# RMSNorm and QKV product on one core: two head tiles transposed by the DMA crossbar among the weight loads, a new order of the head, and the last columns in halves

## Chip, cores and metric

The kernel runs on one core of a Trainium2 chip. The metric is the device time of one execution in microseconds. Each kernel was run several times, unless the text says otherwise. "Span" is the profiled length of one execution on the core.

## The reference

```python
def reference(x, gamma, w_qkv, eps):          # x: 8 x 1024 x 768, w_qkv: 768 x 2304, f32
    rms = np.sqrt(np.mean(x ** 2, axis=-1, keepdims=True) + eps)
    x_norm = x / rms * gamma
    return np.matmul(x_norm, w_qkv).astype(np.float32)
```

The 8192 rows are 64 tiles of 128 rows. The inner dimension of 768 is six blocks of 128, numbered ko 0 to 5.

## The kernel before

The weights arrive in pieces. Each piece is multiplied by gamma and turned into bf16 ("conv"). A tile of x must stand transposed before it can be the stationary operand. Tiles 0 to 2 are transposed on PE in f32, and tiles 3 to 5 on PE in bf16. From tile 6 on, a DMA crossbar transpose does it, issued by SP:

```python
HEAD = 6                       # tiles that share the weights while these arrive
...
def tr(t):                     # on PE, into PSUM; cp copies it to xT
    PT[t] = psum.tile([P, KO, P], bf16, name="pm")
    for ko in range(KO):
        nc.tensor.transpose(out=PT[t][:, ko, :], in_=XB[t][:, ko * P:(ko + 1) * P], identity=ident)
...
def xbar(t):                   # on the DMA engines
    XT[t] = xTp.tile([P, KO, P], bf16, name="xT")
    nc.sync.dma_start_transpose(out=XT[t], in_=XB[t])
```

1/rms is applied to the product, in the eviction from PSUM. A list gives every operation of the head a planned time, and each engine executes its operations in the order of those times. The times are an order, not waits. After the head, a loop plans one tile after another:

```python
for t in range(HEAD, MT):
    ahead = 6.0 if t < HEAD + 5 else 0.0
    ...
    at(now - 15 - ahead, load_x, t)
    at(now - 8.5 - ahead, cast, t)
    at(now - 7.5 - ahead, xbar, t)
    ...
    for n0 in range(0, N, NT):
        at(now, mm, t, n0, range(KO))
        now += min(NT, N - n0) * US
        flip ^= 1
        evac_at(now + 0.2, t, n0, "DVE" if flip else "ACT", gap=1.2)
```

The line with `ahead` matters later: tiles 6 to 10 have a lead of 6 us, and tile 11 is the first without it. All loads, stores and crossbar transposes but one tiny load are issued by SP, in this order of times.

Of the kernel before, what the change touches and what calls it, by code (L numbers as in the profile page):

```python
# [10 lines left out]
HEAD = 6  # L11
PIECES = [(0, 2, 0, 512), (2, 3, 0, 512), (3, 4, 0, 512), (4, 5, 0, 512), (5, 6, 0, 512), (0, 2,
          512, 512), (2, 4, 512, 512), (4, 6, 512, 512), (0, 2, 1024, 512), (2, 4, 1024, 512), (4,
          6, 1024, 512), (0, 3, 1536, 512), (3, 6, 1536, 512), (0, 6, 2048, 256)]


LOADS = [
    (-9.00, "w", 0), (-8.99, "x", 0), (-8.98, "x", 1), (-8.97, "x", 2), (-8.96, "w", 1),
    (-8.95, "w", 2), (-8.94, "w", 3), (-8.93, "x", 3), (-8.92, "w", 4), (-8.91, "w", 5),
    (-8.90, "x", 4), (-8.89, "w", 6), (-8.88, "w", 7), (-8.87, "x", 5), (-8.86, "w", 8),  # L20
    (-8.85, "w", 9), (-8.84, "w", 10), (-8.83, "w", 11), (-8.82, "w", 12), (-8.81, "w", 13),
    (-8.80, "x", 6), (-8.79, "x", 7),
]

EARLY = 3


HEAD_PLAN = [
    (4.99, "conv", 0, 0, "DVE"), (4.99, "conv", 0, 1, "ACT"), (5.95, "trA", 0), (5.99, "stat", 0),
    (6.82, "trB", 0), (7.04, "trB", 1), (7.18, "cpB", 0, "DVE"), (7.25, "trA", 1),  # L30
    (7.26, "idle", 3), (7.32, "cpA", 0, "ACT"), (7.58, "cpB", 1, "DVE"), (7.94, "stat", 1),
    (7.94, "trA", 2), (7.98, "cpA", 1, "DVE"), (8.37, "mm", 0, 0, "01"),
    (8.65, "conv", 1, 2, "POOL"), (8.66, "cpA", 2, "DVE"), (8.80, "mm", 1, 0, "01"),
    (9.24, "trB", 2), (9.27, "stat", 2), (9.34, "conv", 2, 3, "DVE"), (9.45, "mm", 2, 0, "01"),
    (9.82, "recip", 0), (9.89, "mm", 0, 0, "2"), (9.98, "cpB", 2, "DVE"),
    (9.99, "conv", 3, 4, "POOL"), (10.10, "mm", 1, 0, "2"), (10.32, "mm", 2, 0, "2"),
    (10.38, "recip", 1), (10.53, "mm", 0, 0, "3"), (10.66, "recip", 2), (10.75, "mm", 1, 0, "3"),
    (10.97, "mm", 2, 0, "3"), (10.98, "cast", 3, "DVE"), (10.98, "stat", 3),
    (11.18, "mm", 0, 0, "4"), (11.40, "mm", 1, 0, "4"), (11.61, "tr", 3),
    (11.65, "conv", 4, 5, "DVE"), (11.95, "mm", 2, 0, "4"), (12.13, "cp", 3, "DVE"),  # L40
    (12.19, "mm", 0, 0, "5"), (12.41, "mm", 1, 0, "5"), (12.57, "evac", 0, 0, "ACT"),
    (12.63, "mm", 2, 0, "5"), (12.69, "recip", 3), (12.84, "mm", 3, 0, "012345"),
    (12.85, "evac", 1, 0, "DVE"), (13.26, "conv", 5, 0, "ACT"), (13.60, "conv", 5, 1, "DVE"),
    (13.97, "evac", 2, 0, "ACT"), (14.08, "cast", 4, "DVE"), (14.14, "mm", 0, 512, "01"),
    (14.57, "mm", 1, 512, "0"), (14.63, "evac", 3, 0, "DVE"), (14.66, "stat", 4),
    (14.78, "tr", 4), (15.12, "mm", 1, 512, "1"), (15.33, "conv", 6, 2, "POOL"),
    (15.34, "mm", 2, 512, "01"), (15.38, "cp", 4, "DVE"), (15.77, "mm", 3, 512, "01"),
    (15.99, "conv", 6, 3, "ACT"), (16.05, "recip", 4), (16.20, "mm", 4, 0, "012345"),
    (16.70, "conv", 7, 5, "ACT"), (17.41, "conv", 7, 4, "ACT"), (17.49, "mm", 4, 512, "01"),
    (17.65, "evac", 4, 0, "DVE"), (17.93, "mm", 0, 512, "23"), (18.12, "stat", 5),  # L50
    (18.36, "mm", 1, 512, "23"), (18.40, "cast", 5, "DVE"), (18.79, "mm", 2, 512, "23"),
    (19.01, "conv", 8, 0, "DVE"), (19.22, "tr", 5), (19.49, "conv", 8, 1, "DVE"),
    (19.56, "mm", 3, 512, "23"), (19.97, "cp", 5, "DVE"), (19.99, "mm", 4, 512, "23"),
    (20.42, "mm", 0, 512, "45"), (20.53, "conv", 9, 2, "DVE"), (20.85, "mm", 1, 512, "45"),
    (21.01, "conv", 9, 3, "DVE"), (21.01, "evac", 0, 512, "ACT"), (21.28, "mm", 2, 512, "45"),
    (21.49, "evac", 1, 512, "DVE"), (21.69, "conv", 10, 4, "POOL"), (21.70, "conv", 10, 5, "ACT"),
    (21.71, "mm", 3, 512, "45"), (22.15, "mm", 4, 512, "45"), (22.24, "evac", 2, 512, "DVE"),
    (22.41, "evac", 3, 512, "ACT"), (22.58, "mm", 5, 0, "012345"), (22.99, "evac", 4, 512, "DVE"),
    (23.70, "conv", 11, 1, "ACT"), (23.74, "conv", 11, 2, "DVE"), (23.87, "mm", 5, 512, "012345"),
    (24.22, "conv", 11, 0, "DVE"), (24.70, "recip", 5), (24.92, "evac", 5, 0, "DVE"),  # L60
    (25.17, "mm", 0, 1024, "01"), (25.33, "evac", 5, 512, "ACT"), (25.60, "mm", 1, 1024, "01"),
    (25.71, "conv", 12, 3, "DVE"), (26.02, "conv", 12, 5, "ACT"), (26.03, "mm", 2, 1024, "01"),
    (26.19, "conv", 12, 4, "DVE"), (26.46, "mm", 3, 1024, "01"), (26.89, "mm", 4, 1024, "01"),
    (27.33, "mm", 5, 1024, "01"), (27.76, "mm", 0, 1024, "23"), (28.10, "conv", 13, 1, "ACT"),
    (28.10, "conv", 13, 2, "POOL"), (28.10, "conv", 13, 3, "DVE"), (28.19, "mm", 1, 1024, "23"),
    (28.40, "conv", 13, 5, "DVE"), (28.62, "mm", 2, 1024, "23"), (28.65, "conv", 13, 0, "POOL"),
    (28.70, "conv", 13, 4, "DVE"), (29.05, "mm", 3, 1024, "23"), (29.48, "mm", 4, 1024, "23"),
    (29.91, "mm", 5, 1024, "23"), (30.35, "mm", 0, 1024, "45"), (30.78, "mm", 1, 1024, "45"),
    (30.94, "evac", 0, 1024, "DVE"), (31.21, "mm", 2, 1024, "45"),
    (31.37, "evac", 1, 1024, "ACT"), (31.64, "mm", 3, 1024, "45"),  # L70
    (31.80, "evac", 2, 1024, "DVE"), (32.07, "mm", 4, 1024, "45"),
    (32.23, "evac", 3, 1024, "ACT"), (32.50, "mm", 5, 1024, "45"),
    (32.66, "evac", 4, 1024, "DVE"), (32.94, "mm", 0, 1536, "012"),
    (33.10, "evac", 5, 1024, "ACT"), (33.58, "mm", 1, 1536, "012"), (34.23, "mm", 2, 1536, "012"),
    (34.88, "mm", 3, 1536, "012"), (35.53, "mm", 4, 1536, "012"), (36.17, "mm", 5, 1536, "012"),
    (36.82, "mm", 0, 1536, "345"), (37.47, "mm", 1, 1536, "345"), (37.63, "evac", 0, 1536, "DVE"),
    (38.12, "mm", 2, 1536, "345"), (38.28, "evac", 1, 1536, "ACT"), (38.76, "mm", 3, 1536, "345"),
    (38.92, "evac", 2, 1536, "DVE"), (39.41, "mm", 4, 1536, "345"),
    (39.57, "evac", 3, 1536, "ACT"), (40.06, "mm", 5, 1536, "345"),
    (40.22, "evac", 4, 1536, "DVE"), (40.70, "mm", 0, 2048, "012345"),  # L80
    (40.86, "evac", 5, 1536, "ACT"), (41.36, "mm", 1, 2048, "012345"),
    (41.52, "evac", 0, 2048, "DVE"), (42.02, "mm", 2, 2048, "012345"),
    (42.18, "evac", 1, 2048, "DVE"), (42.67, "mm", 3, 2048, "012345"),
    (42.83, "evac", 2, 2048, "DVE"), (43.33, "mm", 4, 2048, "012345"),
    (43.49, "evac", 3, 2048, "DVE"), (43.98, "mm", 5, 2048, "012345"),
    (44.14, "evac", 4, 2048, "DVE"), (44.80, "evac", 5, 2048, "DVE"),
]
HEAD_END = 44.64


@with_exitstack
def kernel(
# [8 lines left out]
    nc = tc.nc  # L101
# [8 lines left out]
    Kw, N = w_qkv.shape  # L110
# [20 lines left out]

    ctx.enter_context(tc.manual_schedule())

    warm = singles.tile([P, NT], bf16)
    nc.vector.memset(warm, 0.0)  # L135
    g6 = singles.tile([KO, P], f32)
    nc.scalar.dma_start(out=g6, in_=gamma.rearrange("(ko p) -> ko p", p=P))
    eps_sb = singles.tile([P, 1], f32)
# [83 lines left out]

    begun = {}

    def mm(t, n0, kos):
        nl = min(NT, N - n0)
        for ko in kos:
            if (t, n0) not in PM:
                PM[t, n0] = psum.tile([P, NT], f32, name="pm")
            b = begun[t, n0] = begun.get((t, n0), 0) + 1  # L230
            nc.tensor.matmul(out=PM[t, n0][:, :nl], lhsT=XT[t][:, ko, :], rhs=w_b[:, ko, n0:n0 + nl],  # L231
                             start=(b == 1), stop=(b == KO))
# [2 lines left out]
        return max(i for i, (p0, _) in enumerate(PARTS) if p0 <= n0)  # L235

    def evac(t, n0, eng):
        nl = min(NT, N - n0)
        h = part(n0)
        if (t, h) not in OUT:  # L240
            OUT[t, h] = outp.tile([P, PARTS[h][1]], f32, name=f"ot{h}")
        o = OUT[t, h][:, n0 - PARTS[h][0]:n0 - PARTS[h][0] + nl]
        pm = PM[t, n0]
        if eng == "DVE":
            nc.vector.tensor_scalar(out=o, in0=pm[:, :nl], scalar1=RS[t], scalar2=None, op0=mult)  # L245
        else:
            nc.scalar.activation(out=o, in_=pm[:, :nl], func=AF.Copy, scale=RS[t], bias=0.0)  # L247
# [9 lines left out]
    def at(time, fn, *args):  # L257
        plan.append((time, len(plan), fn, args))
# [8 lines left out]
    def evac_at(time, t, n0, eng, gap):  # L267
        at(time, evac, t, n0, eng)
        h = part(n0)
        nl = min(NT, N - n0)  # L270
        left[t, h] = left.get((t, h), PARTS[h][1]) - nl
        if t >= MT - 2:
            at(time + gap - 0.5, store, t, h, n0, nl)
        elif left[t, h] == 0:
            at(time + gap, store, t, h, *PARTS[h])

    def idle(n, nl=P):
        wps = psum.tile([P, NT], f32, name="pm")
        for _ in range(n):
            nc.tensor.matmul(out=wps[:, :nl], lhsT=warm[:, :P], rhs=warm[:, :nl], start=True, stop=True)  # L280


    for time, kind, n in LOADS:
        at(time, {"x": load_x, "w": load_w, "t": xbar}[kind], n)
    at(0.0, idle, 4, NT)
    at(2.8, gamma_in)
    at(2.81, idle, 6, NT)
    at(2.82, idle, 3)
    ops = {"conv": conv, "cast": cast, "stat": stat, "recip": recip, "tr": tr, "cp": cp, "mm": mm, "idle": idle}
    for time, op, *args in HEAD_PLAN:  # L290
        if op == "evac":
# [12 lines left out]
    for t in range(HEAD, MT):  # L304
# [5 lines left out]
        at(now - 7.5 - ahead, xbar, t)  # L310
        at(now - 5, stat, t)
        at(now - 3, recip, t)
        for n0 in range(0, N, NT):
            at(now, mm, t, n0, range(KO))
            now += min(NT, N - n0) * US
            flip ^= 1
            evac_at(now + 0.2, t, n0, "DVE" if flip else "ACT", gap=1.2)

# [37 lines left out]
```

## Time and profile before

| | |
|---|---|
| device time, median of all 6 runs beside the change's | 388.91 us (388.61 to 389.31) |
| span of the profiled run | 386.7 us |
| weight piece 4 (the last of columns 0 to 511) landed | 11.43 us |
| last eviction of the head (tile 5) began | 44.78 us |
| last eviction of the kernel began | 383.21 us |
| time per tile between these | 5.835 us |

Two views of the kernel before that the prediction does not show are needed later. The first is the timeline of PE's weight loads from 66 to 76 us, where tile 11 begins (near 74). Its columns are start, length, engine, line, operation, tile, shapes and count; a wait ahead of a load would follow in brackets:

```profile
65.97 10.04 PEld L231 LDWEIGHTS <-xT 128*128 128x128 bf16 x53
```

One unbroken group: PE waited for nothing there. The second view is the last store on SP (duration, first and last start, then its time to landing):

```profile
L251 SPq DMA_DIRECT2D out_dram<-ot x1: 378/378/378, 383.8 to 383.8; - x1
DMA to landing us min/median/max: 2.0/2.0/2.0
```

It was issued 0.56 us after the last eviction began.

### The profile page before, as it was taken

Reading aid. Unit: us, or ns where it says so; the run is one execution under the profiler, and the core shown is the slowest. Engines: PE = TensorE matmul, PEld = TensorE weight load, DVE = VectorE, ACT = ScalarE, POOL = GpSimd, SP = SyncE. Lnnn points to the kernel's source line nnn. Section 1 sums busy time; section 2 is a strip of 40 time slices with the busy share of each in tenths; the row PEclk is TensorE's granted clock in tenths of the full one; section 3 lists DMA queues with packets and bytes.
Section 4 is the critical chain, followed back from the end, with each engine's and each line's share of the span. In section 5 each row is a group of like instructions: output and inputs, shape, how many; then the busy total and the mean of one; then the engine's idle time right before and its main releaser. Section 6 shows DMA issues by size and latency. Waiting matters only on the chain.

```text
span 386.7 us, 5481 instructions
## 1 busy us (share of the span) xinstructions
PE 380.0 (98%) x1935; PEld 193.1 (50%) x1973; DVE 157.0 (41%) x316; ACT 180.5 (47%) x360; POOL 4.6 (1%) x12
## 2 busy tenths in 40 slices
PE   8999999999999999999999999999999999999996
PEld 5444655454554554554554554554554554554553
DVE  3765543334333344333344333343333343333332
ACT  6743444453544443544444444544444534444532
POOL 1101000000000000000000000000000000000000
PEclk9999999999999999999999999999999999999999
DMA  8999999999998999999999999999999999999975
GB/s 294 390 381 341 394 300 354 325 311 321 287 303 279 307 302 338 313 295 321 283 312 302 303 308 295 316 303 294 311 316 293 297 312 316 288 315 299 279 272 189
DMA packets 87943, 119.52 MB, mean 309 GB/s; under 512 B 50790, under 2 KB 59756, under 8 KB 87916
## 3 DMA queue, kind: packets, MB, share of 16 engines
q1 hardware_dynamic: 87904, 119.17, 101.7%
q8 instruction: 15, 0.25, 0.3%
q14 instruction: 12, 0.10, 0.1%
q10 hardware_dynamic: 12, 0.00, 0.0%
HBM read 32.25 MB, written 75.50 MB: 279 GB/s over the span
## 4 chain that ended last, share of the span: by engine, by line
PE 98%; issue 1%; ACT 0%; DVE 0%
PE pm L231 96%; PE pm L280 1%; PE pm L212 1%; PE pm L198 0%; ACT ot L247 0%; DVE warm L135 0%; PE pm L262 0%; DVE eps_sb L139 0%
## 5 line engine op out<-in xcount | busy, mean ns | idle before, releaser
L231 PE MATMUL pm<-w_b,xT 128*128 128x512 bf16 (+1 forms) x1882 | 372.1, 357 | 2.0
L231 PEld LDWEIGHTS <-xT 128*128 128x128 bf16 x1920 | 187.7, 98 | 184.7 <-DVE xT L174 0.5
L245 DVE TENSOR_SCALAR ot<-pm,rstd 128x512 f32<-128x512 f32 (+1 forms) x164 | 113.4, 693 | 213.0 <-PE pm L231 212.7
L247 ACT ACTIVATE ot<-pm,rstd 128x512 f32<-128x512 f32 (+1 forms) x156 | 101.0, 647 | 192.6 <-PE pm L231 137.4
L185 ACT ACTIVATE sq<-x_t 128x768 bf16<-128x768 f32 x64 | 53.4, 834 | 1.0 <-DMA x_t<-in_x_dram 1.0
L174 DVE CAST xb<-x_t 128x768 bf16<-128x768 f32 x61 | 33.1, 543 | 3.6 <-DMA x_t<-in_x_dram 3.6
L187 ACT ACTIVATE rms<-ssq,eps_sb 128x1 f32<-128x1 f32 x64 | 18.8, 294 | 2.1
L185 ACT ACTIVATION_READ_ACCUMULATOR sq<-x_t 128x1 f32 x64 | 12.3, 192 | 0.0
L192 DVE RECIPROCAL rstd<-rms 128x1 f32<-128x1 f32 x64 | 9.7, 153 | 0.0
L168 ACT ACTIVATE w_b<-w_f,g_sb 128x512 bf16<-128x512 f32 (+1 forms) x9 | 6.1, 693 | 6.1 <-DMA w_f<-in_w_qkv_dram 6.1
L166 DVE TENSOR_SCALAR w_b<-w_f,g_sb 128x512 bf16<-128x512 f32 (+1 forms) x15 | 6.8, 486 | 4.5 <-DMA w_f<-in_w_qkv_dram 4.4
L280 PE MATMUL pm<-warm 128*128 128x512 bf16 (+1 forms) x16 | 5.3, 493 | 1.2 <-DVE eps_sb L139 1.2
L170 POOL TENSOR_SCALAR w_b<-w_f,g_sb 128x512 bf16<-128x512 f32 (+1 forms) x6 | 3.9, 652 | 25.3 <-DMA w_f<-in_w_qkv_dram 25.3
L280 PEld LDWEIGHTS <-warm 128*128 128x128 bf16 x16 | 1.8, 131 | 3.4 <-issue 2.2
L174 DVE CAST xT<-pm 128x256 bf16<-128x256 f32 (+1 forms) x5 | 2.4, 527 | 1.9 <-PE pm L212 1.9
L212 PE MATMUL pm<-ident_f,x_t 128*128 128x128 f32 x18 | 2.8, 300 | 0.0
L212 PEld LDWEIGHTS pm<-ident_f,x_t 128*128 128x128 f32 x18 | 2.4, 162 | 0.2
L142 ACT ACT_TABLE_LOAD x1 | 1.3, 1283 | 1.4 <-PEq L337 1.4
L174 DVE COPY xT<-pm 128x768 bf16<-128x768 bf16 x3 | 1.7, 557 | 0.4 <-PE pm L198 0.4
L198 PEld LDWEIGHTS <-xb 128*128 128x128 bf16 x18 | 1.3, 98 | 0.7
L198 PE MATMUL pm<-ident,xb 128*128 128x128 bf16 x18 | 1.5, 219 | 0.0
L263 DVE COPY g_sb<-pm 128x6 f32<-128x6 f32 x1 | 0.2, 164 | 1.7 <-PE pm L262 1.7
(13 smaller groups left out, 2.7 us busy)
## 6 DMA issues: line engine op xcount, KB each, us to landing
out_dram<-ot SPq DMA_DIRECT2D x124, 512.0 KB, 4.0
x_t<-in_x_dram SPq DMA_DIRECT2D x64, 384.0 KB, 4.4
out_dram<-ot SPq DMA_DIRECT2D x64, 128.0 KB, 3.2
w_f<-in_w_qkv_dram SPq DMA_DIRECT2D x7, 512.0 KB, 7.2
w_f<-in_w_qkv_dram SPq DMA_DIRECT2D x3, 768.0 KB, 9.9
out_dram<-ot SPq DMA_DIRECT2D x8, 256.0 KB, 2.0
w_f<-in_w_qkv_dram SPq DMA_DIRECT2D x4, 256.0 KB, 5.9
xT<-xb SPq DMA_TRANSPOSE x58, 4.5
```

What stands on the lines that cost most here:

```text
L166: nc.vector.tensor_scalar(out=o, in0=i, scalar1=g, scalar2=None, op0=mult)
L168: nc.scalar.activation(out=o, in_=i, func=AF.Copy, scale=g, bias=0.0)
L170: nc.gpsimd.tensor_scalar(out=o, in0=i, scalar1=g, scalar2=1.0, op0=mult, op1=mult)
L174: nc.vector.tensor_copy(out=out, in_=in_)
L185: nc.scalar.activation(out=sq, in_=X[t], func=AF.Square, accum_out=ssq)
L187: nc.scalar.activation(out=rms, in_=ssq, func=AF.Sqrt, scale=inv_k, bias=eps_sb)
L192: nc.vector.reciprocal(out=r, in_=RS[t])
L212: nc.tensor.transpose(out=PT[t, h][:, ko - k0, :], in_=X[t][:, ko * P:(ko + 1) * P], identity=ident_f)
L231: nc.tensor.matmul(out=PM[t, n0][:, :nl], lhsT=XT[t][:, ko, :], rhs=w_b[:, ko, n0:n0 + nl], start=(b == 1), stop=(b == KO))
L245: nc.vector.tensor_scalar(out=o, in0=pm[:, :nl], scalar1=RS[t], scalar2=None, op0=mult)
L247: nc.scalar.activation(out=o, in_=pm[:, :nl], func=AF.Copy, scale=RS[t], bias=0.0)
L280: nc.tensor.matmul(out=wps[:, :nl], lhsT=warm[:, :P], rhs=warm[:, :nl], start=True, stop=True)
```

## The change

The intent is to take work off PE in the head, where PE is already the bound, and to shorten the tail. The diff, cut to its core (the head's list is rewritten whole; four lines stand for it):

```diff
-          6, 1024, 512), (0, 3, 1536, 512), (3, 6, 1536, 512), (0, 6, 2048, 256)]
+          6, 1024, 512), (0, 2, 1536, 512), (2, 4, 1536, 512), (4, 6, 1536, 512), (0, 3, 2048,
+          256), (3, 6, 2048, 256)]
 LOADS = [
...
-    (-8.85, "w", 9), (-8.84, "w", 10), (-8.83, "w", 11), (-8.82, "w", 12), (-8.81, "w", 13),
-    (-8.80, "x", 6), (-8.79, "x", 7),
+    (-8.85, "w", 10), (-8.84, "x", 5), (15.52, "t", 4), (15.53, "w", 11), (15.54, "w", 12),
+    (15.55, "w", 13), (22.65, "t", 5), (22.66, "w", 14), (22.67, "w", 15), (22.68, "x", 6),
+    (22.69, "x", 7),
 ]
 HEAD_PLAN = [        # cut
-    (14.78, "tr", 4), ... (15.38, "cp", 4, "DVE"), ... (19.22, "tr", 5), ... (19.97, "cp", 5, "DVE"),
+    ... (23.66, "mm", 4, 0, "012345"), ... (28.41, "mm", 5, 0, "012345"),
 ]
-    warm = singles.tile([P, NT], bf16)
-    nc.vector.memset(warm, 0.0)
+    ones = nc.const_aps.tensor(1.0, [P, NT], bf16)
...
+    def width(t, n0):
+        return P if t == MT - 1 and n0 >= N - 2 * P else min(NT, N - n0)
...
-    at(0.0, idle, 4, NT)
+    at(0.0, idle, 5, NT)
     at(2.8, gamma_in)
     at(2.81, idle, 6, NT)
-    at(2.82, idle, 3)
...
-        for n0 in range(0, N, NT):
+        for n0 in [*range(0, N, NT)] + [N - P] * (t == MT - 1):
```

"t" in the list of loads is a crossbar transpose, "tr" and "cp" are a transpose on PE and the copy of its result. In the changed kernel the four tiles 0 to 3 consume the first 1024 to 1536 columns, and tiles 4 and 5 follow. A side effect of the list is that the first stores of results come after all of these loads.

## The prediction

> **What bounds the kernel now.** I read the page first, the chain that ended last second, then the timeline of the first 30 us, then transfers (issue time and time to landing) and 1 us windows around the first crossbar transposes.
>
> From the page of the kernel before (busy time, chain, the two costliest kinds):
>
> ```profile
> PE 380.0 (98%) x1935; PEld 193.1 (50%) x1973; DVE 157.0 (41%) x316; ACT 180.5 (47%) x360; POOL 4.6 (1%) x12
> PE 98%; issue 1%; ACT 0%; DVE 0%
> L231 PE MATMUL pm<-w_b,xT 128*128 128x512 bf16 (+1 forms) x1882 | 372.1, 357 | 2.0
> L280 PE MATMUL pm<-warm 128*128 128x512 bf16 (+1 forms) x16 | 5.3, 493 | 1.2 <-DVE eps_sb L139 1.2
> L198 PE MATMUL pm<-ident,xb 128*128 128x128 bf16 x18 | 1.5, 219 | 0.0
> ```
>
> TensorE works to the end: the chain is 98% PE, the matmuls waited 2.0 us in all, and no other engine is above half busy. A busy row is no proof of full speed, so I take the pace from the chain and the evictions. Tile 5's last eviction starts at 44.78, PE's last matmul ends at 383.21: (383.21 - 44.78) / 58 tiles = 5.835 us a tile. A tile has 24 matmuls of 512 columns and 6 of 256, i.e. 27 times 512, so 0.2161 us per 512 columns.
>
> The span is therefore: the time until matmuls run without end, plus everything that PE does besides matmuls after that, plus 64 tiles, plus the tail. Only the first, second and last can change. The chain in order of time shows the second:
>
> ```profile
> 11.75 0.34 PE pm L198 x6
> 12.14 2.75 PE pm L231 x12
> 14.89 0.34 PE pm L198 x6
> 15.23 4.10 PE pm L231 x19
> 19.33 0.34 PE pm L198 x6
> 19.66 1.29 PE pm L231 x6
> ...
> 376.09 7.10 PE pm L231 x38
> 383.21 0.47 ACT ot L247
> ```
>
> (start, length, what.) The three 0.34 pieces are the PE transposes of tiles 3, 4 and 5; no waits of size stand around them. The tail is one ACT eviction, a store that lands 2.0 us after its issue, and the end at 386.7.
>
> What feeds the head is the load stream. Issue times plus times to landing give w piece 4 at 11.43, piece 5 at 12.77, piece 7 at 16.47, piece 9 about 20.1, piece 10 at 23.0, piece 11 at 25.0, piece 12 at 27.05, piece 13 at 29.24, x tiles 6 and 7 at 30.2 and 31.2. That is 524 KB per 1.34 us (391 GB/s), with one jump of about 1.5 us between pieces 9 and 10. The timeline shows the jump at the conversion of piece 10:
>
> ```profile
> 23.02 0.72 ACT L168 ACTIVATE w_b<-w_f,g_sb 128x512 bf16<-128x512 f32 x1 [1.33 <-DMA w_f<-in_w_qkv_dram]
> 23.08 0.69 POOL L170 TENSOR_SCALAR w_b<-w_f,g_sb 128x512 bf16<-128x512 f32 x1 [7.18 <-DMA w_f<-in_w_qkv_dram]
> ```
>
> A 16 KB instruction packet occupies one DMA engine for 1.09 us from 19.59; before it the first and last of the 16 completion marks of a load are 0.75 us apart, after it 2.2. So one engine fell behind and each landing waits for it.
>
> **What the Trainium skill says.** "Runtime: NRT & Kernel Launch", section Instruction fetch mechanics: instructions are refilled in blocks of 16 KiB, 256 instructions, through DMA. The trace agrees in size and spacing: such packets stand at 19.59, 44.3, 65.2, 89.9 us, and PE executes some 256 loads and matmuls in 25 us (255 and 258 in the 50 us from 50). "TensorE: Matmul & The Clock Gate", section on 56 ns against 53.3: warm start-to-start is 55.6 ns at 128 columns and 215.7 at 512. The trace has 0.34 / 6 = 57 ns and 216 ns. "DMA: Bandwidth & Descriptors", section DMA Transpose (X-bar): a transpose next to ordinary transfers needs nothing, two transposing streams must not overlap. All here are issued by SP, so it is one stream. The page gives no cost for one among loads; the trace does, below.
>
> **The change part by part.**
>
> 1. Tiles 4 and 5 leave PE. Removed from PE: two pieces of 0.34, 0.68 us, all on the path. DVE also loses two copies of 0.56, off the path. In their place SP issues two crossbar transposes, costed as a rival below.
>
> 2. The first matmuls. Up to the fourth single-ko piece both kernels wait for the same bytes (the order of loads is the same to piece 5), and 15 matmuls of ko 0 to 4 for three tiles are due before piece 4 is converted. It lands at 11.43, DVE needs 0.49, after the cast of tile 3: ready about 12.0. Before, PE begins ko 5 at 12.14 + 0.22 (tile 2's ko 4 stands behind the transpose) = 12.36, so PE was late by 0.3. After, the fp32 transposes begin when the warm-up ends and all 15 come before tile 3's transpose, with three filler matmuls behind; ko 5 begins about 12.15. Gain 0.2 us.
>
> 3. Constant ones. The memset of 0.27 us goes, PE begins near 0.85 instead of 1.19; warm-up has 11 matmuls of 512 before x instead of 10 and some small ones. At the cold 0.43 us it ends near 5.95 instead of 6.26, just after x tile 0 (5.69). This feeds part 2 and is not counted twice.
>
> 4. Last columns in halves. 12 matmuls of 128 columns at 57 ns, 0.68, replace 6 of 256, 0.65: +0.03. The last eviction is 128 wide on DVE instead of 256 on ACT. DVE takes 0.75 for 512 and 0.48 for 256, 1.05 ns a column, so about 0.35: 0.12 less than 0.47. A store of 64 KB instead of 128 may land a little sooner; SP's issue of the other half (0.33 to 0.38 us) may delay it. Together -0.1 to -0.2.
>
> 5. Smaller late pieces. Total bytes equal; the first part of the late columns lands earlier. No direct time on PE.
>
> Sum without new waits: -0.68 - 0.20 + 0.03 - 0.15 = -1.00 us.
>
> **The new waits.** After the change PE has four tiles, not six, for the middle columns, so the loads have less time. From ko 5 at 12.15, 53 matmuls of 512 (3 + 6 + 24 for columns 512 to 1023 + 20 for columns 1024 to 1535) precede tile 4: 12.15 + 53 x 0.216 = 23.6. Before that PE needs piece 6 at 15.8 (lands 14.1, worked out at 391 GB/s from piece 5), piece 7 at 17.5 (16.5), piece 8 at 19.3 (17.8), piece 9 at 21.0 (19.15), piece 10 at 22.7 (20.5), each plus a conversion of 0.5 to 0.7. All fit, piece 7 with least room. Tile 5's load lands about 21.5, the transpose of tile 4 behind it 22.2 to 23.7. Tile 5 is wanted 22 matmuls later, 28.35; pieces 11 to 13 (4.0 us) and the second transpose come before it, about 27.5 to 28.7. I put expected waits at 0.25 us.
>
> **The rivals.**
>
> A. The crossbar stops the load stream for longer than its own work, and PE waits. For it, the windows around the first two transposes of the kernel before (columns: PE, PEld, DVE, ACT, POOL busy, clock, DMA share, GB/s):
>
> ```profile
> 35.00:36.00 1.00, 1.00 (x6) 0.49 (x5) 0.00 (x0) 0.00 (x0) 0.00 (x0) 1.00 0.99 406
> 36.00:37.00 1.00, 1.00 (x7) 0.41 (x6) 0.00 (x0) 0.00 (x0) 0.00 (x0) 1.00 2.56 270
> 37.00:38.00 1.00, 1.00 (x6) 0.47 (x5) 0.38 (x1) 0.00 (x0) 0.00 (x0) 1.00 0.44 44
> 38.00:39.00 1.00, 1.00 (x7) 0.46 (x5) 0.46 (x2) 0.69 (x1) 0.00 (x0) 1.00 0.86 213
> ```
>
> Throughput falls from 406 to 44 GB/s. Against it: landings move little. The store ahead landed at 38.66, the transpose at 39.45 (+0.8), the next load at 40.45, the second transpose at 41.1 (+0.65); the engines that were ahead waited for the one behind, whose schedule sets landings anyway. If each costs 2 us instead of 0.75, tile 4 arrives near 24.9 and tile 5 near 31, PE waits 1.3 and 1.3 more, and the time is about 390.5.
>
> B. The instruction packet lands in the tight stretch. PE has 17 instructions fewer in all and lacks two transposes' worth (24) in the head, so the block end that stood at 19.6 comes near 21.5, beside tile 5's load and the first transpose. It delays one engine 1.1 to 1.5 us; tile 4 then lands up to 23.7 or 24.2, a wait of 0.1 to 0.6: 388.5 to 388.9.
>
> C. The gain is hidden: if the head ended when the last weights land, the saved PE time would return as a wait. Against: before, piece 13 lands at 29.24 and its columns are wanted only near 41; after, its columns 1536 up begin at 32.2 with pieces 11 to 13 landed by 28. Loads are late for tiles 4 and 5 alone. It would give 389.
>
> D. Stores start later (behind all loads), so tile 6's transpose could be late. Before it landed at 39.45 and was needed at 44.8; five stores and 1.3 us more leave over 3 us of room. Discounted.
>
> **Range and chances.** 389.05 - 1.00 + 0.25 = 388.3. Before's runs spread 388.73 to 389.31, a median moves about 0.2. Half of B's upper case and a faster tail give 387.7 to 389.0; A in full lies outside. The change cannot reach 2% (7.8 us) unless PE's pace changed, and a loss of that size needs several waits of 2 us and more: 0.01 each, 0.98 within.
>
> **What would show it right or wrong.** Right: 0.34 pieces of bf16 transposes once instead of three times; ko 5 begins near 12.15; tile 5's 256-wide eviction starts near 44.0 instead of 44.78; a last eviction of about 0.35 on DVE; 5.835 us a tile unchanged. Wrong: PE weight loads or matmuls that wait for the crossbar's transfer near 23.6 or 28.4 by over 0.5 us (A, B), a conversion of pieces 7 to 10 that PE waits for, or a clock lower than 1.00 after the changed warm-up.

## The result

| | before | changed |
|---|---|---|
| device time, median | 388.91 us | 388.46 us |
| lowest to highest | 388.61 to 389.31 (6 runs) | 388.12 to 389.87 (6 runs) |
| ratio to before | | 0.9993, 95% interval 0.9977 to 1.001 |
| span of the profiled run | 386.7 us | 386.9 us |

A ratio is the mean time of one kernel's runs over that of the other's in the same rounds, so it is not quite the ratio of the two medians. The time lies in the predicted range, and the class is "same". The medians differ by 0.45 us, but one run at 389.87 pulls the mean back. The profiled run of the changed kernel is no shorter than that of before. So the question is where a predicted gain of 1.00 us, less 0.25 of waits, went.

The page of the changed kernel, in answer to the lines of before (busy time, chain, matmuls, crossbar waits):

```profile
PE 379.9 (98%) x1927; PEld 192.2 (50%) x1965; DVE 153.4 (40%) x307; ACT 181.6 (47%) x365; POOL 6.5 (2%) x14
PE 89%; DMA 8%; issue 1%; DVE 1%; ACT 1%; SPq 0%
L235 PE MATMUL pm<-w_b,xT 128*128 128x512 bf16 (+1 forms) x1888 | 372.1, 357 | 2.1
L235 PEld LDWEIGHTS <-xT 128*128 128x128 bf16 x1926 | 187.9, 98 | 185.5 <-DMA xT<-xb 0.5
```

PE's busy time is unchanged to 0.1 us. What is new is that the chain has 8% of DMA in it, and that weight loads waited for a crossbar transpose. The chain in order of time shows the route (start, length, what):

```profile
16.13 6.01 DMA x_t<-in_x_dram
22.14 0.02 issue
22.16 0.57 DVE xb L174
22.73 0.02 issue
22.75 6.20 DMA xT<-xb
28.95 0.05 issue
28.99 6.00 PE pm L235 x27
```

Before, nothing but PE stood in this stretch. Now tile 5's load, its cast and its crossbar transpose set when PE goes on. The timeline of the weight loads has the wait itself, and PE's own timeline has the start of the head:

```profile
28.99 50.92 PEld L235 LDWEIGHTS <-xT 128*128 128x128 bf16 x273 [0.55 <-DMA xT<-xb]
```

```profile
11.98 0.51 PE L198 MATMUL pm<-ident,xb 128*128 128x128 bf16 x6
12.32 0.34 PE L284 MATMUL pm<-const-bfloat16-1.0 128*128 128x128 bf16 x3
12.59 47.72 PE L235 MATMUL pm<-w_b,xT 128*128 128x512 bf16 x238
```

The bf16 transposes stand once instead of three times, as foreseen. But ko 5 begins at 12.59, later than the 12.36 of before. In this execution x tile 1 landed at 7.33 (6.68 before) and weight piece 4 at 12.02 (11.43 before), although both kernels issue the same loads in the same order up to there. One DMA engine had fallen behind: of the 16 completion marks of x tile 1, fifteen had come by 6.45 and the last came at 7.33. So a single profile of each kernel cannot be compared by the clock alone. Tile 5's last eviction began at 44.79, to be compared with 44.78. The kernel before has one profile only; with 388.6 us it was among the fastest of its runs.

The tail, in the view of SP's last stores:

```profile
L255 SPq DMA_DIRECT2D out_dram<-ot x2: 383/392/401, 383.8 to 384.2; - x2
DMA to landing us min/median/max: 1.6/1.6/1.6
```

The last store is now issued at 384.24, 1.01 us after the last eviction began (383.23), instead of 0.56. It lands 1.6 us later instead of 2.0.

### The profile page after: what moved, and what is told of

Same layout as the page of the kernel before. It is cut to its first block, busy times and chain, and to the rows that moved or that the text cites. A ratio compares the mean times of both kernels' runs of the same rounds, so it can differ in the third digit from the quotient of the medians.

```text
span 386.9 us, 5470 instructions
## 1 busy us (share of the span) xinstructions
PE 379.9 (98%) x1927; PEld 192.2 (50%) x1965; DVE 153.4 (40%) x307; ACT 181.6 (47%) x365; POOL 6.5 (2%) x14
## 4 chain that ended last, share of the span: by engine, by line
PE 89%; DMA 8%; issue 1%; DVE 1%; ACT 1%; SPq 0%
PE pm L235 89%; DMA x_t<-in_x_dram 3%; DMA w_f<-in_w_qkv_dram 2%; DMA xT<-xb 2%; DMA out_dram<-ot 1%; ACT ot L251 1%; DVE ot L249 0%; DVE xb L174 0%; SPq L160 0%; SPq L155 0%; SPq L255 0%; ACT w_b L168 0%
## 5 line engine op out<-in xcount | busy, mean ns | idle before, releaser
L249 DVE TENSOR_SCALAR ot<-pm,rstd 128x512 f32<-128x512 f32 (+1 forms) x161 | 111.5, 695 | 206.1 <-PE pm L235 201.7
L251 ACT ACTIVATE ot<-pm,rstd 128x512 f32<-128x512 f32 (+2 forms) x160 | 102.7, 643 | 191.7 <-PE pm L235 151.0
L166 DVE TENSOR_SCALAR w_b<-w_f,g_sb 128x512 bf16<-128x512 f32 (+1 forms) x16 | 7.7, 499 | 5.9 <-DMA w_f<-in_w_qkv_dram 5.9
L170 POOL TENSOR_SCALAR w_b<-w_f,g_sb 128x512 bf16<-128x512 f32 (+1 forms) x8 | 5.8, 735 | 23.5 <-DMA w_f<-in_w_qkv_dram 23.5
L284 PE MATMUL pm<-const-bfloat16-1.0 128*128 128x512 bf16 (+1 forms) x14 | 5.4, 539 | 0.8 <-PEq L340 0.8
L168 ACT ACTIVATE w_b<-w_f,g_sb 128x512 bf16<-128x512 f32 (+1 forms) x6 | 3.6, 612 | 2.7 <-DMA w_f<-in_w_qkv_dram 2.7
L284 PEld LDWEIGHTS <-const-bfloat16-1.0 128*128 128x128 bf16 x14 | 1.5, 126 | 2.7 <-issue 2.7
L176 ACT CAST xT<-pm 128x256 bf16<-128x256 f32 (+1 forms) x5 | 2.3, 458 | 0.9 <-PE pm L212 0.7
L174 DVE COPY xT<-pm 128x768 bf16<-128x768 bf16 x1 | 0.6, 557 | 0.0
```

The source lines that it names most:

```text
L166: nc.vector.tensor_scalar(out=o, in0=i, scalar1=g, scalar2=None, op0=mult)
L168: nc.scalar.activation(out=o, in_=i, func=AF.Copy, scale=g, bias=0.0)
L170: nc.gpsimd.tensor_scalar(out=o, in0=i, scalar1=g, scalar2=1.0, op0=mult, op1=mult)
L174: nc.vector.tensor_copy(out=out, in_=in_)
L249: nc.vector.tensor_scalar(out=o, in0=pm[:, :nl], scalar1=RS[t], scalar2=None, op0=mult)
L251: nc.scalar.activation(out=o, in_=pm[:, :nl], func=AF.Copy, scale=RS[t], bias=0.0)
```

## The experiments

Twelve kernels were run, in three groups that each share their runs of the kernel before. Every one was correct. The table puts the times and the profiles side by side; the sections after it take the kernels one by one. "Head" is the start of tile 5's last eviction less the landing of weight piece 4 in the same execution. This takes out the chance of the first loads, since up to that landing all kernels issue the same loads. "Tile 11" is the distance between the last evictions of tiles 10 and 11, less 5.84 us: what PE waited there. (The waits of weight loads, which the views show in brackets, are about 0.1 us longer.) The diffs below are cut to what was changed.

| kernel | median us | before, same rounds | ratio (95% interval) | piece 4 landed | head | tile 11 |
|---|---|---|---|---|---|---|
| before | | | | 11.43 | 33.35 | 0 |
| changed | 388.46 | 388.91 | 0.9993 (0.9977 to 1.001) | 12.02 | 32.77 | 0 |
| e1_repeat | 388.51 | 388.70 | 0.9998 (0.9986 to 1.0009) | 11.56 | 32.81 | 1.03 |
| e2_tail_whole | 388.12 | 388.70 | 0.9983 (0.9971 to 0.9996) | 11.74 | 32.76 | 0.22 |
| e3_two_queues | 388.46 | 388.70 | 0.9995 (0.9984 to 1.0007) | 11.65 | 32.78 | 0.91 |
| e4_t5_early | 389.47 | 388.70 | 1.0031 (1.0003 to 1.0059) | 11.54 | (a) | 1.16 |
| e5_tile11_ahead | 388.23 | 388.71 | 0.9988 (0.9975 to 1.0) | 11.34 | 33.01 | (b) 0 |
| e6_pe_transposes | 388.32 | 388.71 | 0.9990 (0.9978 to 1.0003) | 11.52 | 33.22 | 0 |
| e7_best | 388.05 | 388.71 | 0.9983 (0.997 to 0.9995) | 11.46 | 33.03 | (b) 0 |
| e8_best_t5 | 388.08 | 388.71 | 0.9979 (0.9966 to 0.9993) | 11.38 | (a) | (b) 0 |
| e9_more_fillers | 388.11, one run | 388.66 | none | 11.43 | 32.83 | 0 |
| e10_pe_whole | 388.59 | 388.66 | 1.0001 (0.9989 to 1.0014) | 11.76 | 33.20 | 0 |
| e11_zeros | 388.70 | 388.66 | 0.9997 (0.9984 to 1.001) | 11.49 | 32.81 | 0 |
| e12_old_pieces | 388.33 | 388.66 | 0.9989 (0.9974 to 1.0003) | 11.51 | 32.89 | 0.44 |

(a) The later evictions of the head stand in another order of time there, so this measure does not hold. (b) Read from the weight loads, which do not wait there.

### e1_repeat: the changed kernel again

The edit is none.

> The changed kernel as it is, for a second profile and more times beside the kernel before. In its first profile the matmuls of ko 5 began at 12.66 us (12.36 before the change), because one DMA engine ran 0.6 us behind from the second x tile on. Theory: that early lag is chance of one execution, not of the change; then here x tile 1 lands near 6.7 and not 7.3, and ko 5 begins near 12.15. The PE wait for tile 5's crossbar transpose near 28.4 us (0.55 us) recurs, since the instruction packet behind the first transpose recurs near 22 us. Rival: the early lag belongs to the change and shows again. Time: 388.2 to 388.7, ratio 0.998 to 0.9995.

Measured: x tile 1 landed at 6.87 and piece 4 at 11.56, so the early lag was chance, as the theory said. Ko 5 began at 12.12. (The 12.66 of the expectation is 12.59 in the trace.) The ratio of 0.9998 is just above the expected range. The wait for tile 5's transpose recurred. But the profile holds a wait that neither theory had. The weight loads of the second profile:

```profile
28.57 44.66 PEld L235 LDWEIGHTS <-xT 128*128 128x128 bf16 x240 [0.59 <-DMA xT<-xb]
74.36 5.73 PEld L235 LDWEIGHTS <-xT 128*128 128x128 bf16 x30 [1.14 <-DMA xT<-xb]
```

At the start of tile 11 PE waited again, for tile 11's crossbar transpose. The chain of this execution names it:

```profile
66.33 7.99 DMA xT<-xb
74.32 0.05 issue
74.36 0.39 PE pm L235
```

The transpose was issued at 66.33 and took 7.99 us to land. In the kernel before it was issued at 66.64 and took 4.8, and PE came to tile 11 only near 74. So here the head ended 0.41 us sooner (44.37 instead of 44.78), and tile 11 took back 1.03. In the first profile of the changed kernel the head was late by chance, PE came to tile 11 no sooner than before, and the transpose (67.23 plus 5.85) was there in time. Over the profiles that share this stretch its landing moved from 71.95 (e9) to 74.32 (here), so one profile could miss the wait.

### e2_tail_whole: the last 256 columns whole again

```diff
-        return P if t == MT - 1 and n0 >= N - 2 * P else min(NT, N - n0)
+        return min(NT, N - n0)
...
-        for n0 in [*range(0, N, NT)] + [N - P] * (t == MT - 1):
+        for n0 in range(0, N, NT):
```

> The changed kernel with the last 256 columns of the last tile whole again, as before the change. Theory: halving them gains nothing, since SP then issues three stores one behind another after the last matmuls and the last issue starts 1.0 us after PE's end instead of 0.55; so here the last store is issued 0.55 us after the last matmul ends, and the stretch from the last matmul's end to the end of the span shrinks by about 0.1 us against the changed kernel (3.5 instead of 3.6). Rival, the change's intent: the narrower eviction and smaller store save 0.1 to 0.2 us, so this stretch grows by that much.

Measured in the landing marks of the trace: from the start of the last eviction to the last landing it is 2.51 us before the change and 2.51 here, against 2.62 in the changed kernel and 2.63 in its repeat. So the halves cost 0.12 us, and the rival falls. The kernel's median is 0.39 us below the repeat's in the same rounds, more than the tail explains. Its wait at tile 11 was only 0.22 in the profile. Whether it was small in all its runs is not known.

### e3_two_queues: one of the last stores issued by ACT

```diff
-        nc.sync.dma_start(out=..., in_=...)
+        eng = nc.scalar if (t == MT - 1 and n0 == N - 2 * P) else nc.sync
+        eng.dma_start(out=..., in_=...)
```

> The changed kernel with the store of the first half issued from ACT, which has just evicted it, and the other stores from SP. Theory: SP's row of issues is the cost; the last issue starts right after the last eviction, about 0.5 us after PE's end instead of 1.0, and lands 1.6 us later: the tail is 0.4 to 0.5 us shorter than the changed kernel's. Rival: completion of the stores in flight sets the end, and then the tail moves by less than 0.1 us.

Measured: the last issue did come 0.53 us after the last eviction began, not 1.01. The last landing came 2.67 us after it, no sooner than the 2.62 of the changed kernel:

```profile
L256 SPq DMA_DIRECT2D out_dram<-ot x2: 332/358/383, 383.9 to 384.3; - x2
L256 ACTq DMA_DIRECT2D out_dram<-ot x1: 399/399/399, 383.9 to 383.9; - x1
...
DMA to landing us min/median/max: 2.1/2.3/2.4
```

Issued sooner, the stores took 2.1 to 2.4 us instead of 1.6. My theory that SP's row of issues is the cost falls. What the transfers do after issue sets the end, as the rival said. The trace shows that the last rows of 512 bytes leave the DMA engines 2.22 us after the last eviction's start here, 2.27 in the changed kernel, and that the last rows of 1024 bytes leave after 2.16 before the change. Why they leave no sooner is not shown.

### e4_t5_early: tile 5's transpose ahead of weight pieces 12 and 13

```diff
-    (15.53, "w", 11), (15.54, "w", 12), (15.55, "w", 13), (22.65, "t", 5),
+    (15.53, "w", 11), (22.651, "w", 12), (22.652, "w", 13), (22.65, "t", 5),
```

> The changed kernel with tile 5's crossbar transpose ahead of weight pieces 12 and 13 instead of behind them. Theory: its place behind two pieces of 1.35 us, together with the late landing behind the first transpose, makes PE wait 0.55 us near 28.4; here it lands near 26.3 to 26.9, PE does not wait there, and tile 5 ends 0.5 us sooner than in the changed kernel; pieces 12 and 13 land near 27.5 and 29 and are wanted from 34 on. Rival: the crossbar so early leaves the transfer queue empty while SP waits for the cast, pieces 11 to 13 land over 2 us later and PE waits for them near 32 to 37 instead; no gain.

Measured: the transpose landed at 25.80 and the wait near 28.4 was gone, as the theory said. Pieces 12 and 13 landed at 27.8 and 29.2 and nobody waited for them, so the rival's mechanism did not show. Still the kernel was slower than before. The weight loads:

```profile
19.97 53.06 PEld L235 LDWEIGHTS <-xT 128*128 128x128 bf16 x278
74.32 5.73 PEld L235 LDWEIGHTS <-xT 128*128 128x128 bf16 x30 [1.29 <-DMA xT<-xb]
```

PE runs from 20 us without a break, and then waits 1.29 us at tile 11. In this execution whatever the head saves, tile 11 takes back. One of the six runs took 393.13; the others took 388.69 to 389.65, against 388.61 to 388.90 before.

### e5_tile11_ahead: a lead of 6 us for tile 11 too

```diff
-        ahead = 6.0 if t < HEAD + 5 else 0.0
+        ahead = 6.0 if t < HEAD + 6 else 0.0
```

> The changed kernel with one more tile, the eleventh, loaded, cast and transposed 6 us earlier. Theory: the head's gain (tile 5 ends 0.3 to 0.4 us sooner) is given back at the start of tile 11 near 73.3 us, whose crossbar transpose lands 73.7 to 74.4 us because the transfers run some 3 us further behind than before the change and tile 11 is the first without the 6 us of lead; here PE does not wait there, the last matmul ends 0.3 to 0.9 us sooner than in the repeat, and the median falls to about 388.1. Rival: the queue, not the lead, is short; then another tile (12 or 13) waits as long and nothing is gained.

Measured: no wait at tile 11, nor at tiles 12 and 13. The weight loads:

```profile
23.80 4.43 PEld L235 LDWEIGHTS <-xT 128*128 128x128 bf16 x22 [0.80 <-DMA xT<-xb]
28.47 47.55 PEld L235 LDWEIGHTS <-xT 128*128 128x128 bf16 x254 [0.24 <-DMA xT<-xb]
```

The last eviction began at 382.80, which is 1.04 us sooner than in the repeat and 0.41 sooner than before. The head had ended 0.43 sooner than before, so this time the gain of the head reached the end. The median is 388.23. Tile 11's transpose landed at 66.19, some 7 us before PE came to it. The lead was what was short, and the rival falls. The ratio's interval overlaps the repeat's, so the profile shows this and not the median. The wait at tile 11 differs between executions of one kernel from nothing to over 1 us. That fits the changed kernel's wide spread of times: the profiled runs with waits of 1.03 (e1) and 0.91 (e3) took 389.26 and 389.24, each the slowest of its five, and those of e9 and e11, without a wait, took 388.11 and 388.17. The unprofiled runs show only their totals.

### e6_pe_transposes: tiles 4 and 5 on PE again, all else as changed

```diff
-    (15.52, "t", 4), (22.65, "t", 5),
+    (17.15, "tr", 4), (17.16, "cp", 4, "DVE"), ... (23.22, "tr", 5), (23.225, "cp", 5, "DVE"),
```

> The changed kernel with tiles 4 and 5 transposed on PE again (two crossbar transposes taken out of the loads, everything else kept). Theory: PE gets 0.68 us of transposes back, loses the wait near 28.4 (0.3 to 0.55 us), and since the loads and stores are 1.5 us further on, the wait at tile 11 falls to under 0.3 us: the time is within 0.3 us of the changed kernel's. Rival: the crossbar part alone carries the change's gain in full; then this kernel is 0.7 us slower than the changed one.

Measured: 388.32, within 0.2 us of the changed kernel, with no wait for a crossbar in the head and none at tile 11. Its head is 33.22. The changed order with the crossbar has 32.76 to 32.89 in seven profiles (mean 32.81), and before has 33.35. In these seven the two crossbar transposes shorten the head by 0.41 us, and of the 0.68 us that left PE, 0.27 came back as waits. The profiles of e5 and e7 have the same head and 33.01 and 33.03: the weight loads waited 0.8 us at tile 4 there, the gain is 0.20 and 0.48 came back. The rest of the change is worth 0.13 us by the one profile of the kernel before.

### e7_best and e8_best_t5: both losses taken away

```diff
-        ahead = 6.0 if t < HEAD + 5 else 0.0
+        ahead = min(6.0, max(0.0, HEAD + 11.0 - t))
```

The last columns are whole as in e2_tail_whole. The second kernel has e4's order of loads as well.

> The changed kernel with whole last columns and a lead of 6 us that is kept for tile 11 and falls by 1 us a tile to tile 17. Theory: both losses are taken away, the gain of the head stays to the end: 387.9 to 388.1, 0.6 to 0.8 us below the kernel before, clear of its interval. Rival: moving transposes forward makes other tiles wait; then over 388.3.

> The same with tile 5's transpose ahead of pieces 12 and 13, which by itself made the kernel slower (389.47) though the wait near 28.4 was gone. Theory: that loss sits at tile 11 (its wait was 1.1 us there) and perhaps at its neighbours, so with the lead it goes away and the saved 0.3 us shows: 387.6 to 387.9. Rival: the loss sits in the head or in the stores; then it stays above the kernel without this move, 388.2 or more.

Measured: 388.05 and 388.08, with intervals of 0.997 to 0.9995 and 0.9966 to 0.9993 to the kernel before, both clear of 1. PE waits at no tile from 11 to 16 in either. So e4's loss sat at tile 11, as expected: with the lead it is gone. The second expectation failed: the 0.3 us of wait that the earlier place saves do not show in the time. Where they went I did not find out. Their ratios to before are 0.9983 and 0.9979; the changed kernel has 0.9993 and, repeated, 0.9998. They were not run in the same rounds as the changed kernel, and the intervals overlap. Nor does the time show that both losses had to go: e2, with whole columns and without the lead, has 0.9983 as well. That the waits at tile 11 are gone is shown by the profiles.

### e9_more_fillers: 24 more PE instructions ahead of the work

```diff
-    at(0.0, idle, 5, NT)
+    at(0.0, idle, 1, NT)
+    at(0.01, idle, 16)
```

> The changed kernel with four of the five first filler matmuls of 512 columns cut into sixteen of 128: the same columns, 24 more PE instructions ahead of all work. Theory: the 16 KB packet comes with PE's 256-instruction blocks, so it moves 12 pairs of 0.216 us, 2.6 us, earlier, to 19.0 to 19.6, and the loads that land from then on to the first crossbar transpose (w piece 10 and x tile 5, or x tile 5's transpose) are the late ones: the first transpose lands near 23.8 and not 22.6, and piece 11 comes 1.35 us behind it, not 2.6. Rival: the late landing behind the first transpose belongs to the crossbar; then piece 11 is still 2.6 us behind the transpose.

This tests rival B of the prediction, the instruction packet. In the changed kernel a 16 KB packet stood at 22.20 us and in the repeat at 21.77, and weight piece 11 landed 2.65 and 2.63 us behind tile 4's transpose. Two landings of such pieces are otherwise 1.34 us apart. Here the packet moved to 18.50 (19.0 to 19.6 was expected). Tile 5's load landed at 22.86 (21.69 in the repeat), the transpose at 23.66 (22.52), and piece 11 at 25.03, now 1.37 behind the transpose. So the extra 1.3 us follows the packet and does not belong to the crossbar. The timeline of DVE shows the shift, the repeat first and then this kernel:

```profile
21.71 0.56 DVE L174 CAST xb<-x_t 128x768 bf16<-128x768 f32 x1 [1.34 <-DMA x_t<-in_x_dram]
```

```profile
22.88 0.56 DVE L174 CAST xb<-x_t 128x768 bf16<-128x768 f32 x1 [2.67 <-DMA x_t<-in_x_dram]
```

What moves is which landing is late. From piece 11 on all is as before, within the 0.13 us by which piece 4 differs. This was one look at one run, of unknown state; it is used for the order of landings only.

### e10_pe_whole: PE transposes and whole last columns

The edits of e6_pe_transposes and e2_tail_whole together.

> The changed kernel with tiles 4 and 5 transposed on PE and whole last columns: what is left of the change is its new order of the head, the ones and the pieces. Theory: the crossbar part is worth nothing as it stands, because its 0.68 us come back as waits, so this is at 388.1 to 388.2, as the crossbar kernel with whole columns (388.12). Rival: the crossbar part pays; then this one is 0.3 us or more slower than that kernel, 388.4 or above.

Measured: 388.59, so the number expected by the rival. Its profile has the head of e6 (33.20 and 33.22) and no waits at tile 11. One of its six runs took 390.14. By these rounds the crossbar transposes are worth 0.47 us (388.59 less 388.12, with the two kernels in different rounds); by e1 and e6 they cost 0.19. Both pairs differ in nothing but the transposes, so times of this size do not decide it. The heads of the profiles do, with 0.4 us for the crossbar in seven and 0.2 in two, as long as tile 11 does not take it back.

### e11_zeros: zeros from a memset instead of constant ones

```diff
-    ones = nc.const_aps.tensor(1.0, [P, NT], bf16)
+    ones = singles.tile([P, NT], bf16)
+    nc.vector.memset(ones, 0.0)
```

> The changed kernel with the memset of zeros back in place of the constant ones, the fillers as changed. Theory: PE starts at 1.2 instead of 0.77 us, the fillers end 0.3 to 0.4 us later, near 6.2, still ahead of what the head waits for (weight piece 4 near 11.4), so ko 5 begins at the same distance from that landing (0.63 us) and the time is that of the changed kernel within 0.2 us. Rival: the earlier start is part of the gain; then it is 0.3 us slower.

Measured: PE began at 1.19 instead of 0.77 us and the head is 32.81, the same. The ratio is 0.9997 beside the repeat's 0.9998. The earlier start buys nothing, because the head waits for weight piece 4.

### e12_old_pieces: the late weight pieces as before

```diff
-          6, 1024, 512), (0, 2, 1536, 512), (2, 4, 1536, 512), (4, 6, 1536, 512), (0, 3, 2048,
-          256), (3, 6, 2048, 256)]
+          6, 1024, 512), (0, 3, 1536, 512), (3, 6, 1536, 512), (0, 6, 2048, 256)]
```

The lists of loads and conversions are adapted to these pieces.

> The changed kernel with the late weight pieces as before (two of 3 x 512 and one of 6 x 256 instead of three of 2 x 512 and two of 3 x 256). Theory: their columns are wanted from 32 us on and land by 29, so the size of the pieces does not reach PE; the wait at tile 5 stays at 0.2 to 0.6 us and the time is the changed kernel's within 0.2 us. Rival: fewer, larger pieces [...]move the transposes; then the waits of PE change by over 0.3 us.

Measured: 388.33 and a head of 32.89, within 0.1 us of the others. It had a wait at tile 11 of 0.44. Its weight loads waited 0.68 us at tile 4 and 0.28 at tile 5, where the changed kernel's waited 0.55 at tile 5 alone, so the rival's 0.3 is passed. But e5 and e7, with the smaller pieces, show the same pattern (0.80 and 0.24, 0.82 and 0.25). The smaller pieces are worth nothing that these runs can see.

## Why the prediction was right, and where it was not

The time and the class were right. In part this was luck: the range of 387.7 to 389.0 holds the 388.91 of the kernel before, so a change worth nothing would have landed in it too. The sum was right in its largest term and wrong in three others. Tile 5's last eviction, foreseen near 44.0, came at 44.79, and at 44.37 in the repeat. Two slips moved nothing: 383.21 is the start of the last eviction (PE ended at 383.18), and the pages count 16 PE instructions fewer, not 17.

**Part 1, two transposes off PE (-0.68), with waits of 0.25 in their place: right in the main.** In seven profiles the head with the crossbar is 0.41 us shorter than without it, so 0.27 us of waits came back. In e5 and e7 it was 0.48.

**The cost of a crossbar transpose among loads (0.75 us), against rival A's 2 us: right.** Tile 5's load landed at 22.14 and tile 4's transpose at 22.92 in the first profile; weight piece 13 landed at 28.26 and tile 5's transpose at 28.94. That is 0.78 and 0.68 us. With against without gives a little more: from piece 4 to piece 14 it took 18.07 to 18.26 us in eight profiles with the two transposes among the same pieces, and 16.28 and 16.46 in e6 and e10, so 0.8 to 1.0 us for each. Throughput falls as rival A said, and yet landings move little. The windows of the changed kernel (PE, PEld, DVE, ACT and POOL busy, clock, DMA share, GB/s):

```profile
26.00:27.00 1.00, 1.00 (x6) 0.46 (x5) 0.36 (x2) 0.18 (x1) 1.00 (x3) 1.00 2.76 251
27.00:28.00 1.00, 1.00 (x6) 0.48 (x5) 0.39 (x1) 0.50 (x1) 0.95 (x2) 1.00 0.07 21
28.00:29.00 1.00, 0.94 (x6) 0.22 (x4) 0.71 (x2) 0.71 (x2) 0.00 (x0) 1.00 1.07 292
```

Throughput drops to 21 GB/s, but the 16 completion marks of the load ahead now come within 0.1 us of each other (28.16 to 28.26) instead of 1.4. So the slowest engine, which sets the landing, loses little more than the 0.7 us of the transpose.

**Rival B, the instruction packet beside the first transpose: right.** It was predicted near 21.5 and stood at 22.20, 1.04 us long, and in the other profiles of the same PE order at 21.46 to 21.92. Where it came at 21.46 to 21.57 (e5, e7, e8), and in e12 at 21.66, tile 4's transpose was the late one, and weight loads waited 0.5 to 0.8 us at tile 4. Elsewhere (21.66 to 22.20) the delay passed to piece 11 and to tile 5's transpose, and they waited 0.55 to 0.60 us near 28.4, but for e4, where that transpose comes sooner. Both are past the 0.5 us which the prediction named as a sign against it.

**Part 2, the first matmuls (-0.20): too large by the end of the head.** Ko 5 began 0.57 us after piece 4 landed instead of 0.93, which is more than foreseen. But by the end of the head only 0.13 was left in the two kernels without the crossbar. Where the other 0.2 went I did not isolate. Its absolute time, "near 12.15", depended on the landing of piece 4, which moved between 11.34 and 12.02 from one profile to another. That is as much as the whole effect, and the prediction had given it no spread.

**Part 4, the tail (+0.03 - 0.15): the sign was wrong.** The narrower eviction took 0.35 us as said. I had counted SP's issue as a maybe. It did come 0.45 us later, and the smaller store landed only 0.34 us sooner after issue. The sum is +0.11 us, or +0.12 in the repeat.

**Rival D, stores later, so a later transpose is late: this was the step that failed, as "Discounted".** A transpose was late, but at another tile. I checked tile 6, the next one, and found over 3 us of room. The kernel's room runs out where its lead does, at tile 11. Seven profiles share the changed order of that stretch: the changed kernel, e1, e2, e3, e9, e11 and e12. There tile 11's transpose took 5.5 to 8.0 us to land, against 4.8 before, while PE arrived up to 0.5 us sooner. The waits are 0, 1.03, 0.22, 0.91, 0, 0 and 0.44 us, 0.37 on average. That the missing lead lets the wait happen is shown by e5. That the longer landing comes from the stores which start behind the head's loads was argued and not tested alone.

The traces hold a second candidate, which the experiments left out. In e1 the load ahead of tile 11's transpose had 15 of its 16 completion marks by 69.42 and the last at 72.35; in e9 it had them by 69.07 and 69.98. So one DMA engine was behind, and throughput was low until it was done. The same microsecond in e1 and in e9, with the columns as above:

```profile
71.00:72.00 1.00, 1.00 (x6) 0.45 (x5) 0.00 (x0) 0.00 (x0) 0.00 (x0) 1.00 0.06 23
```

```profile
71.00:72.00 1.00, 1.00 (x7) 0.46 (x5) 0.52 (x1) 0.00 (x0) 0.00 (x0) 1.00 1.11 388
```

A later 16 KB instruction packet stands near. It began at 66.65 and 67.45 in e9 and e11 (no wait), at 68.10 and 68.30 in e2 and the changed kernel (0.22 and 0), and at 68.96, 68.98 and 69.51 in e3, e12 and e1 (0.91, 0.44, 1.03). No run moved this packet alone, and an engine that is behind might also start it late. So this is a coincidence in seven profiles and not a cause shown.

The balance for the changed kernel as the profiles have it: head -0.54 (32.81 less 33.35), tail +0.12, tile 11 +0.37, together -0.05 us. With e5 and e7 among the heads it is -0.50 for the head and -0.01 in all, and the head of before rests on one profile. The ratios of the two rounds, 0.9993 and 0.9998, are -0.27 and -0.08 us of 388.9 and 388.7. They agree with each other and with this within their intervals.

Parts 3 and 5, the ones and the pieces, were held to be worth nothing, and e11 and e12 agree.

## What to carry to other kernels

When a change makes an early stage shorter, follow the engine onward to the first place where its supplies have the least lead, not only to the next one: the gain ends where the slack ends. Look at more than one profile of each kernel, and measure a stage from the event that feeds it rather than from the start of the clock, before half a microsecond is given a cause. A narrower last store is not a shorter tail; what counts is the last landing.

## What the Trainium skill lacked or had wrong

- "DMA: Bandwidth & Descriptors", section DMA Transpose (X-bar): it names no cost of a crossbar transpose among ordinary loads. Here one of 128 x 768 bf16 landed 0.68 and 0.78 us behind the load ahead of it, and two put a later load back by 0.8 to 1.0 us each, while throughput falls to 21 GB/s in one microsecond and the completion marks of the transfer ahead draw together to 0.1 us.
- "Runtime: NRT & Kernel Launch", section Instruction fetch mechanics: it calls the cost of crossing a 16 KiB boundary mostly hidden. For PE's own instructions that holds here (in the kernel before PE has no wait above 0.15 us from 13 us on). But in the head the block takes 1.00 to 1.09 us of one DMA engine. In e1 the load in flight landed 1.3 us later for it, and in the kernel before the completion marks of a load stood 2.2 us apart after it instead of 0.75.
- "TensorE: Matmul & The Clock Gate", section Back-to-back issue gap: it gives about 131 ns a matmul of 512 columns and 81 ns of 128 in a stream with weight loads. This stream has 216 ns, and the last twelve matmuls of 128 columns start 56 ns apart, each with its own weight load. These are the values that the section gives for an isolated matmul.
- No page that I read says how far the first loads of one kernel differ between executions: the same weight piece landed at 11.34 to 12.02 us over fourteen profiles.
